# A hybrid encoder layer: the sample's first activations from a channel-major copy of the input and a tile of inverse norms, without transposes on TensorE

## Chip, cores and metric

The kernel runs on one core of one Trainium2 chip. The metric is device time in microseconds, the median of repeated executions. Engines are TensorE (PE in the profile; PEld are its weight loads), VectorE (DVE), ScalarE (ACT), GpSimd (POOL) and SyncE (SP), whose queue issues all transfers of this kernel. SBUF is the on-chip memory, PSUM the memory into which TensorE writes.

## The reference

One encoder layer is applied with the same weights to two groups: the prompt (512 tokens) and the sample (1024 tokens), each of 1024 channels in fp32. What the change touches is the first line of it, for the sample:

```python
h = rms_norm(x, g_pre_mix) * (1.0 + sc1) + sh1
u = h @ w_in
```

where `rms_norm(x, g) = x * rsqrt(mean(x*x over channels) + eps) * g`. The norm is one number per token; `g`, `sc1` and `sh1` are one number per channel. After it come five projections of `h`, a gated linear recurrence, a Fourier branch, a merge with an output projection and a residual, and then a channel sub-layer with a convolution.

## The kernel before

Products on TensorE want the contracted channels on the partitions, so `h` is held channel-major: eight tiles `h` of 128 channels x 1024 tokens for the sample. To keep fp32 accuracy each operand is split in two tiles of the type fp32r, a high part (`hh`, `ah`, and half of an `hl` weight tile) and a low part (`hl`, `al`), and each product is made of three passes: high x high, high x low, low x high (`fm_mm`, `km_mm`, `passes`). `split` (lines 105 to 112) makes the high part by a Copy on ScalarE (line 109, `act=True`) or by a cast on VectorE (line 111), and the low part by a subtract on VectorE (line 112).

The program is a list of `Step`s that `emit` (line 176) writes out in order. A step has loads, written five steps ahead of it (`LOAD_AHEAD`); a weight unit, loaded into one of three `raw` tiles and split three units ahead (`AHEAD`), into one of four `hl` tiles; the matmuls `mm`; and what follows them, `post`. `defer(fn, 1)` puts an operation to the end of the next step. The order in which each engine works is the order in which its instructions were written. A tile comes from a pool of 40 `big` buffers and is taken when one is free.

`h_steps` (line 436) makes `h` from rows of tokens in two lists of steps:

- list a, eight steps: load 128 rows (`x`), Square with a row sum on ScalarE (line 413), mean and power -0.5 on POOL (`rstd`, lines 430 and 431), and one step later the rows scaled by the inverse norm on ScalarE (`xn`, line 418).
- list b, eight steps: eight 128x128 transposes of `xn` on TensorE into PSUM (`trans`, line 204), the modulation on ScalarE (Identity with a scale and a bias per channel, line 461), the cast and the subtract on VectorE, and a store of `h` to `hrow` for the Fourier branch.

`h_steps` serves four places. The one that changes is the sample's first sub-layer. Its list a is woven into the first half of the prompt's 16 merge steps (units `w_a` and `w_b`; `weave` puts one after each), beside steps that make the gates by products on VectorE (`ada`, line 337). Its list b is woven into the prompt's eight output-projection steps (`rows_steps`, units `w_o`), one ahead of each; the texts call these R0 to R7. Ahead of each R step, three units ahead, the operands of a later one are split: activations `ah` and `al` from `mg`, and the weight tile. After R3 and after R7 four PSUM results are evicted: four Squares on ScalarE (line 1080), four products with the gate on VectorE (line 1088, `ro<-ps,gate`). Behind R7 comes the first projection of the sample, `w_xa`, 48 matmuls that walk through the eight pairs `hh`, `hl` in order; the texts call it F0. Its result goes to ScalarE at line 650.

Of the kernel before, what the change touches and what calls it, by code (L numbers as in the profile page):

```python
# [11 lines left out]
F32R = mybir.dt.float32r  # L12
AF = mybir.ActivationFunctionType
ALU = mybir.AluOpType
# [4 lines left out]
KT = D // 128  # L19
# [53 lines left out]
class Enc:  # L73
# [359 lines left out]
    def h_steps(self, sq, src, sub, box, quads=False):  # L433
        nc = self.nc
        xn = []
        box["hi"], box["lo"] = [], []
        rows = []

        def ld(t):
            def f():  # L440
                x = self.big([128, 1024], name="x")
                nc.sync.dma_start(out=x, in_=src[t * 128:(t + 1) * 128, :])
                rows.append(x)
            return f

        def norm(t):
            return lambda: xn.append(self.norm_rows(rows[t], True))

        def tr(g):
            def f():  # L450
                ps = self.ps([128, sq.nf, sq.n])
                for i in range(sq.nf):
                    k = g * sq.nf + i
                    for t in range(sq.tt):
                        self.trans(
                            ps[:, i, t * 128:(t + 1) * 128], xn[t][:, k * 128:(k + 1) * 128], self.ident)
                n = sq.n
                h = self.big([128, sq.nf, n], name="h")
                for i in range(sq.nf):
                    k = g * sq.nf + i  # L460
                    nc.scalar.activation(
                        out=h[:, i, 0:n], in_=ps[:, i, :], func=AF.Identity,
                        scale=self.gs[:, sub, sq.idx, k:k + 1], bias=self.mod[:, 3 * sub, sq.idx, k:k + 1])
                if quads:
                    blocks(h)
                    return
                hi = self.big([128, sq.nf, n], F32R, name="hh")
                lo = self.big([128, sq.nf, n], F32R, name="hl")
                self.split(hi, lo, h)
                for i in range(sq.nf):  # L470
                    box["hi"].append(hi[:, i, :])
                    box["lo"].append(lo[:, i, :])
                if sub == 0:
                    self.defer(lambda: nc.sync.dma_start(
                        out=self.hrow[sq.name][g * sq.nf:(g + 1) * sq.nf].rearrange("k p n -> p k n"), in_=h), 1)

            def blocks(h):
                for c in range(2):
                    t = self.big([128, 2, 512], F32R, name="hx")
                    self.split(t[:, 0, :], t[:, 1, :], h[:, 0, c * 512:(c + 1) * 512])  # L480
                    box.setdefault((g // 4, c), []).append(t)
            return f
        a = [Step(loads=[ld(t)], post=norm(t)) for t in range(sq.tt)]
        b = [Step(mm=tr(g)) for g in range(sq.groups)]
        return a, b


# [893 lines left out]
def weave(main, side, at, stride):  # L1381
    out = []
    side = list(side)
    for i, s in enumerate(main):
        if i >= at and (i - at) % stride == 0 and side:
            out.append(side.pop(0))
        out.append(s)
    return out + side


def place(main, side, at):
    out = []
    side = list(side)
    at = sorted(at)
    for i, s in enumerate(main):
        while at and at[0] <= i and side:
            at.pop(0)
            out.append(side.pop(0))
        out.append(s)
    return out + side  # L1400


@with_exitstack
def encoder(ctx: ExitStack, tc: tile.TileContext, a, outs):
    nc = tc.nc
    e = Enc(ctx, tc, a, outs)
    p, s = e.p, e.s
    x2 = {q.name: e.dram([q.n, D], "x2" + q.name) for q in (p, s)}
    sig = {q.name: {(w, g): e.dram([128, 1024], f"sg{q.name}{w}{g}") for w in range(2) for g in range(q.groups)}
           for q in (p, s)}  # L1410
    with tc.manual_schedule():
        e.setup()
        h1 = {"p": {}, "s": {}}
        h2 = {"p": {}, "s": {}}
        hs = {q: {} for q in "ps"}
        yb = {q: {} for q in "ps"}
        pq = {q: {} for q in "ps"}
        z = {q: {} for q in "ps"}
        mg = {q: {} for q in "ps"}
        gate = {(q, i): {} for q in "ps" for i in range(2)}  # L1420
        fo = {q: {} for q in "ps"}

        def mix(q, heads):
            at = 4
            out = heads[:at] + e.pq_steps(q, pq[q.name], heads[:at]) + heads[at:]
            out += e.ya_steps(q, h1[q.name], hs[q.name], yb[q.name])
            out += e.dft_steps(q, pq[q.name], z[q.name])
            return out

        first, heads = e.mix_heads(p, h1["p"], hs["p"], sig["p"], lead=3)  # L1430
        side = [e.cond_step()] + e.ada_steps(2) + [Step(), Step()] + e.gate_steps(p, 0, gate["p", 0])
        steps = mix(p, heads)
        ya = len(steps) - 10
        sa, sbt = e.h_steps(s, a["x_sample"], 0, h1["s"])
        steps += weave(e.merge_steps(p, yb["p"], z["p"], sig["p"], mg["p"]), sa, 1, 1)
        steps = place(steps, side, [ya - 10] + [ya - 4 + i for i in range(16)] + [ya + 13] + [ya + 22] * 9)
        steps += weave(e.rows_steps(p, a["w_o"], mg["p"], gate["p", 0], a["x_prompt"], x2["p"]), sbt, 0, 1)

        _, heads = e.mix_heads(s, h1["s"], hs["s"], sig["s"])
        steps += place(mix(s, heads), e.ada_steps(3) + e.ada_steps(4), [0, *range(8, 37), *range(36, 46)])  # L1440
        pa, pbt = e.h_steps(p, x2["p"], 1, h2["p"])
        steps += weave(e.merge_steps(s, yb["s"], z["s"], sig["s"], mg["s"]),
                       e.gate_steps(s, 0, gate["s", 0]) + pa, 8, 1)
        steps += weave(e.rows_steps(s, a["w_o"], mg["s"], gate["s", 0], a["x_sample"], x2["s"]), pbt, 4, 2)

        steps += weave(e.up_steps(p, h2["p"], fo["p"]),
                       e.ada_steps(5) + [Step()] * 2 + e.gate_steps(p, 1, gate["p", 1]), 2, 1)
        sa, sbt = e.h_steps(s, x2["s"], 1, h2["s"], quads=True)
        steps += weave(e.rows_steps(p, a["w_down"], fo["p"], gate["p", 1], x2["p"], outs[0]),
                       sa + sbt, 0, 1)  # L1450
        fs = e.dram([FT, 128, 1024], "fs")
        steps += place(e.up_quads(s, h2["s"], fs, 3), e.quad_sums(h2["s"]), [0, 1, 2, 2, 3, 3, 4, 4])
        steps += weave(e.rows_steps(s, a["w_down"], fo["s"], gate["s", 1], x2["s"], outs[1], last=True, fsrc=fs),
                       e.gate_steps(s, 1, gate["s", 1]), 4, 1)

        e.begin(steps)
        e.lead_in(p, a["x_prompt"], first, h1["p"], (2, 2, 2, 2))
        e.emit()
        e.flush()
# [31 lines left out]
def _fm(w):  # L1491
    k, m = w.shape
    return np.ascontiguousarray(w.reshape(k // 128, 128, m // 128, 128).transpose(2, 1, 0, 3)).reshape(m // 128, 128, k)
# [12 lines left out]
def layouts(i):  # L1506
    f = {k: np.asarray(v) for k, v in i.items()}
    o = {"x_prompt": f["x_prompt"][0], "x_sample": f["x_sample"][0]}
    wi = f["w_in"][0]
    o["w_xa"], o["w_ya"] = _fm(wi[:, 0:1024]), _fm(wi[:, 1024:2048])  # L1510
    o["wxbT"] = np.ascontiguousarray(wi[:, 2048:2560].T).reshape(4, 128, 1024)
# [11 lines left out]
    for g in range(GRP):  # L1523
        r = slice(63 * g, 63 * g + 63)
# [45 lines left out]
```

## Time and profile before

| | |
|---|---|
| median of 3 runs (lowest to highest) | 2103.09 us (2102.49 to 2103.74) |
| the profiled execution | 2103.23 us |
| its span, first to last instruction | 2101.1 us |
| mean granted TensorE clock | 0.997 |
| busy: PE, DVE, ACT, POOL | 2068.3, 1420.8, 944.8, 55.3 us |
| transposes of `xn` on PE in the whole kernel | 192, of which 64 belong to the place that changes |

Times in rows are in us from the start of the span. A row of a timeline has the start, the duration, engine, line, operation, output <- inputs, the tile's shape and the count of instructions merged into it; in square brackets stands the idle time of the engine just before it and what ended it. Instructions of one kind on one engine overlap a little, so the distance from start to start can be shorter than the duration.

### The profile page before, as it was taken

How to read it: one execution, taken by the hardware profiler on the slowest of the kernel's cores; microseconds unless marked ns; L12 is line 12 of the kernel's file. 1: busy time of each engine (PE TensorE's matmuls, PEld its weight loads, DVE VectorE, ACT ScalarE, POOL GpSimd, SP SyncE). 2: the span in 40 equal slices, each digit the busy share in tenths (PEclk: the TensorE clock that was granted, in tenths of full speed). 3: DMA queues.
4: the chain of work that ended last, by engine and by line, in shares of the span. 5: the costliest groups of instructions: out<-in, count | busy, mean ns of one | idle time of the engine just before them, and what ended most of it. 6: DMA issues, size and time to landing. Idle time of an engine off the chain costs nothing.

```text
span 2101.1 us, 24339 instructions
## 1 busy us (share of the span) xinstructions
PE 2068.3 (98%) x9602; PEld 1687.5 (80%) x9602; DVE 1420.8 (68%) x1798; ACT 944.8 (45%) x1213; POOL 55.3 (3%) x132
## 2 busy tenths in 40 slices
PE   7999999999999999999999999999999999999998
PEld 6777778888888888888888888888888888888887
DVE  4677888677667664656576445749687887875553
ACT  2377555355565632135333336633344444454442
POOL 0000010000000000000100001000000000000000
PEclk9999999999999999999999999999999999999999
DMA  9643475632233314343543324332122222284422
GB/s 342 206 131 130 145 259 188 236 135 96 100 105 99 112 50 145 121 146 122 217 147 116 111 96 166 100 123 88 61 76 83 83 81 81 100 313 165 143 92 109
DMA packets 91121, 284.57 MB, mean 135 GB/s; under 512 B 9056, under 2 KB 20736, under 8 KB 91008
## 3 DMA queue, kind: packets, MB, share of 16 engines
q1 hardware_dynamic: 91008, 283.03, 39.3%
q8 instruction: 75, 1.23, 0.2%
q14 instruction: 38, 0.31, 0.0%
HBM read 237.87 MB, written 45.12 MB: 135 GB/s over the span
## 4 chain that ended last, share of the span: by engine, by line
PE 87%; DVE 5%; ACT 4%; issue 2%; DMA 2%; POOL 0%; SPq 0%; DVEq 0%; POOLq 0%; ACTq 0%
PE ps L201 86%; PE ps L204 1%; DVE hl L112 1%; ACT th L684 1%; ACT th L694 1%; DVE xc L658 1%; ACT ea L692 1%; DMA hr<-hrowp 1%; ACT xn L413 0%; DVE th L715 0%; DVE th L720 0%; DVE th L718 0%; DMA x<-in_x_sample_dram 0%; DMA x<-in_x_prompt_dram 0%; ACT hl L109 0%
## 5 line engine op out<-in xcount | busy, mean ns | idle before, releaser
L201 PE MATMUL ps<-hh,hl 128*128 128x512 f32 x2144 | 632.6, 394 | 3.5 <-DVE hl L112 3.0
L201 PEld LDWEIGHTS ps<-hh,hl 128*128 128x128 f32 x2144 | 402.2, 188 | 99.5 <-DVE hl L112 4.3
L201 PE MATMUL ps<-hl,ah 128*128 128x512 f32 x1440 | 452.3, 395 | 0.0
L112 DVE TENSOR_TENSOR hl<-raw,hl 128x1024 fp32r<-128x1024 f32 (+2 forms) x240 | 286.8, 1200 | 172.3 <-ACT hl L109 170.8
L201 PE MATMUL ps<-hl,hl 128*128 128x512 f32 x1072 | 380.8, 394 | 0.0
L201 PE MATMUL ps<-hx,wq 128*128 128x512 f32 x1596 | 370.9, 394 | 0.0
L109 ACT ACTIVATE hl<-raw 128x1024 fp32r<-128x1024 f32 (+1 forms) x222 | 232.5, 1053 | 279.3 <-PE ps L201 235.2
L201 PEld LDWEIGHTS ps<-hx,wq 128*128 128x128 f32 x1596 | 299.7, 188 | 71.0 <-DVE wq L1251 0.2
L201 PEld LDWEIGHTS ps<-hl,ah 128*128 128x128 f32 x1440 | 269.0, 188 | 61.8
L201 PE MATMUL ps<-hl,al 128*128 128x512 f32 x720 | 283.9, 394 | 0.0
L201 PEld LDWEIGHTS ps<-hl,hl 128*128 128x128 f32 x1072 | 201.4, 188 | 47.6
L201 PEld LDWEIGHTS ps<-hl,al 128*128 128x128 f32 x720 | 135.2, 188 | 32.0
L1347 DVE SCALAR_TENSOR_TENSOR cf<-ps,vec,cf 128x511 f32<-128x511 f32 (+1 forms) x100 | 75.3, 808 | 83.7 <-ACT cf L1339 83.5
L201 PE MATMUL ps<-yh,hl 128*128 128x512 f32 x384 | 111.8, 394 | 0.6 <-DVE yb L991 0.3
L1250 ACT ACTIVATE wq<-wsum 128x512 fp32r<-128x512 f32 x76 | 46.1, 629 | 118.0 <-DVE wsum L1261 118.0
L1195 DVE SCALAR_TENSOR_TENSOR cf<-cq,vec,cf 128x1023 f32<-128x1023 f32 x76 | 97.1, 1277 | 0.0
L1339 ACT ACTIVATE cf<-ps,vec 128x512 f32<-128x512 f32 (+1 forms) x50 | 39.1, 827 | 105.8 <-PE ps L201 105.8
L201 PEld LDWEIGHTS ps<-yh,hl 128*128 128x128 f32 x384 | 71.5, 188 | 17.6 <-DVE yb L991 0.8
L112 DVE TENSOR_TENSOR al<-fq,ah 128x512 fp32r<-128x512 f32 x88 | 57.2, 686 | 32.3 <-PE ps L201 18.4
L201 PE MATMUL ps<-hx,hl 128*128 128x512 f32 x288 | 66.9, 394 | 0.0
L201 PE MATMUL ps<-yl,hl 128*128 128x512 f32 x192 | 65.3, 394 | 0.0
L658 DVE SCALAR_TENSOR_TENSOR xc<-ps,vec,xc 128x511 f32<-128x511 f32 (+3 forms) x48 | 46.9, 1012 | 25.7 <-ACT xc L650 25.1
(182 smaller groups left out, 2325.0 us busy)
## 6 DMA issues: line engine op xcount, KB each, us to landing
raw<-in_w_up_dram SPq DMA_DIRECT2D x88, 512.0 KB, 3.5
raw<-in_w_down_dram SPq DMA_DIRECT2D x66, 512.0 KB, 3.5
ada<-in_w_adaT_dram SPq DMA_DIRECT2D x32, 512.0 KB, 4.9
raw<-in_w_o_dram SPq DMA_DIRECT2D x24, 512.0 KB, 3.5
fs<-cf SPq DMA_DIRECT2D x22, 512.0 KB, 2.6
fq<-fs SPq DMA_DIRECT2D x22, 512.0 KB, 6.0
ada<-in_w_ada_dram SPq DMA_DIRECT2D x16, 512.0 KB, 8.5
raw<-in_w_gb_dram SPq DMA_DIRECT2D x16, 512.0 KB, 4.3
```

The costliest lines, as they stand in the source:

```text
L109: nc.scalar.activation(out=hi, in_=src, func=AF.Copy)
L112: nc.vector.tensor_tensor(out=lo, in0=src[:, 0:keep], in1=hi[:, 0:keep].bitcast(F32), op=ALU.subtract)
L201: self.nc.tensor.matmul(*args, **kw)
L204: self.nc.tensor.transpose(*args)
L658: nc.vector.scalar_tensor_tensor(out=xc[:, f, o], in0=ps[:, f, o.start + d:o.stop + d], scalar=w[:, tap:tap + 1], in1=xc[:, f, o], op0=ALU ...
L684: nc.scalar.activation(out=t[:, f, :], in_=ps[:, f, :], func=AF.Tanh, scale=0.5, bias=self.halfb[:, b:b + 1])
L692: nc.scalar.activation(out=ea[:, f, :], in_=r[:, f, :], func=AF.Exp, scale=self.nk4[:, k:k + 1], bias=self.nk4[:, k:k + 1])
L694: nc.scalar.activation(out=r[:, f, :], in_=r[:, f, :], func=AF.Tanh, scale=self.k2[:, k:k + 1], bias=self.k2[:, k:k + 1])
L1195: nc.vector.scalar_tensor_tensor(out=box[key][:, o], in0=c[:, i], scalar=self.vec[:, V_FW + 3 * m + t:V_FW + 3 * m + t + 1], in1=box[key][ ...
L1250: nc.scalar.activation(out=hi, in_=src, func=AF.Copy)
L1339: nc.scalar.activation(out=acc[:, f, :], in_=ps[:, f, :], func=AF.Identity, scale=w[:, 1:2], bias=self.vec[:, V_FB + m:V_FB + m + 1])
L1347: nc.vector.scalar_tensor_tensor(out=acc[:, f, o], in0=ps[:, f, o.start + d:o.stop + d], scalar=w[:, tap:tap + 1], in1=acc[:, f, o], op0=A ...
```

## The change

The sample's first sub-layer uses a new function, `ht_steps`, in place of `h_steps`. The host also hands over the sample transposed: `x_sampleT`, eight tiles of 128 channels x 1024 tokens.

- List a keeps load, Square (now in place) and POOL's norm. The scaling of the rows is gone. Instead the 128 norms of a tile are stored to a row in DRAM (`rrow`, elements of 4 bytes), one step later; after the last one, all 1024 norms are loaded as a tile `rb`, the same row on every partition.
- List b has no matmuls. Each of its eight steps has a load of a channel tile, five steps ahead, and as its `post`: a product with `rb` on VectorE, the modulation on ScalarE, and the split with the Copy on ScalarE (it was a cast on VectorE) and the subtract on VectorE. The store to `hrow` stays.

```diff
+        def norm(t):
+            def f():
+                ss = self.small()
+                rs[t] = self.small()
+                x = rows[t]
+                nc.scalar.activation(out=x, in_=x, func=AF.Square, accum_out=ss)
+                self.rstd(rs[t], ss)
+                self.defer(lambda: nc.sync.dma_start(out=rrow[t:t + 1, :].rearrange("o p -> p o"), in_=rs[t]), 1)
+                if t == sq.tt - 1:
+                    self.defer(back, 1)
+            return f
+
+        def back():
+            rows.clear()
+            box["r"] = self.big([128, n], name="rb")
+            nc.sync.dma_start(
+                out=box["r"], in_=rrow.rearrange("(o t) p -> o (t p)", o=1).to_broadcast([128, n]))
+
+        def ldt(k):
+            def f():
+                x = self.big([128, n], name="xt")
+                nc.sync.dma_start(out=x, in_=srcT[k])
+                cols.append(x)
+            return f
+
+        def make(k):
+            def f():
+                h = cols.pop(0)
+                nc.vector.tensor_tensor(out=h, in0=h, in1=box["r"], op=ALU.mult)
+                nc.scalar.activation(out=h, in_=h, func=AF.Identity, scale=self.gs[:, 0, sq.idx, k:k + 1],
+                                     bias=self.mod[:, 0, sq.idx, k:k + 1])
+                hi = self.big([128, n], F32R, name="hh")
+                lo = self.big([128, n], F32R, name="hl")
+                self.split(hi, lo, h, act=True)
+                box["hi"].append(hi)
+                box["lo"].append(lo)
+                self.defer(lambda: nc.sync.dma_start(out=self.hrow[sq.name][k], in_=h), 1)
...
+        a = [Step(loads=[ld(t)], post=norm(t)) for t in range(sq.tt)]
+        b = [Step(loads=[ldt(k)], post=make(k)) for k in range(KT)]
         return a, b
...
-        sa, sbt = e.h_steps(s, a["x_sample"], 0, h1["s"])
+        sa, sbt = e.ht_steps(s, a["x_sample"], a["x_sampleT"], h1["s"])
...
+    o["x_sampleT"] = np.ascontiguousarray(f["x_sample"][0].T).reshape(8, 128, 1024)
```

## Rows read from the trace of the kernel before

**Rows 1.** The page's part 1: busy time, share and instructions of the engines.

```profile
PE 2068.3 (98%) x9602; PEld 1687.5 (80%) x9602; DVE 1420.8 (68%) x1798; ACT 944.8 (45%) x1213; POOL 55.3 (3%) x132
```

**Rows 2.** Timeline of TensorE, the R steps.

```profile
335.91 1.04 PE L204 MATMUL ps<-ident,xn 128*128 128x128 f32 x8
336.70 0.71 PE L201 MATMUL ps<-hl,ah 128*128 128x512 f32 x2
...
337.48 0.62 PE L201 MATMUL ps<-hl,ah 128*128 128x512 f32 x2
...
387.45 0.62 PE L201 MATMUL ps<-hh,hl 128*128 128x512 f32 x2
```

**Rows 3.** Timeline of ScalarE: the first Square after R3, and F0's result.

```profile
360.45 0.60 ACT L1080 ACTIVATE junk<-ps 128x512 f32<-128x512 f32 x1 [2.83 <-PE ps L201]
...
398.75 1.21 ACT L650 ACTIVATE xc<-ps,vec 128x1024 f32<-128x1024 f32 x1 [8.69 <-PE ps L201]
```

**Rows 4.** Timeline of VectorE: a subtract behind ScalarE's copy, in the Fourier branch.

```profile
411.95 1.23 DVE L112 TENSOR_TENSOR el<-eo,eh 128x1024 fp32r<-128x1024 f32 x1 [1.13 <-ACT eh L109]
```

**Rows 5.** Timelines of ScalarE, VectorE, TensorE and SyncE, the merge stage.

```profile
312.53 1.15 ACT L418 ACTIVATE xn<-x,sm 128x1024 f32<-128x1024 f32 x1 [1.26 <-POOL sm L431]
...
321.65 1.06 ACT L109 ACTIVATE hl<-raw 128x1024 fp32r<-128x1024 f32 x1 [3.24 <-DMA raw<-in_w_a_dram]
322.88 1.06 ACT L109 ACTIVATE hl<-raw 128x1024 fp32r<-128x1024 f32 x1 [0.17 <-DMA raw<-in_w_a_dram]
...
314.66 1.23 DVE L112 TENSOR_TENSOR hl<-raw,hl 128x1024 fp32r<-128x1024 f32 x1 [2.85 <-ACT hl L109]
...
315.94 0.73 PE L201 MATMUL ps<-yh,hl 128*128 128x512 f32 x2 [0.29 <-DVE hl L112]
...
315.92 1.14 SPq L124 DMA_DIRECT2D raw<-in_w_a_dram  x2
```

**Rows 6.** Landing of the gate row's store (line 370), and issues by line: its broadcast load.

```profile
DMA to landing us min/median/max: 2.5/2.8/3.1
...
gate<-grow SPq DMA_DIRECT2D x4, 512.0 KB, 6.2
```

**Rows 7.** Timeline of VectorE, the R steps and after.

```profile
341.26 1.23 DVE L112 TENSOR_TENSOR al<-mg,ah 128x1024 fp32r<-128x1024 f32 x1 [1.13 <-ACT ah L109]
342.41 1.22 DVE L112 TENSOR_TENSOR hl<-raw,hl 128x1024 fp32r<-128x1024 f32 x1
343.54 0.69 DVE L111 CAST hh<-h 128x1024 fp32r<-128x1024 f32 x1
...
364.54 1.22 DVE L112 TENSOR_TENSOR al<-mg,ah 128x1024 fp32r<-128x1024 f32 x1
...
375.86 1.23 DVE L112 TENSOR_TENSOR hl<-raw,hl 128x1024 fp32r<-128x1024 f32 x1 [3.38 <-ACT hl L109]
...
422.26 3.92 DVE L658 SCALAR_TENSOR_TENSOR xc<-ps,vec,xc 128x1022 f32<-128x1022 f32 x3 [4.19 <-ACT xc L650]
```

**Rows 8.** Durations (ns) of like operations; ScalarE's timeline of two dependent ones.

```profile
L1187 ACT ACTIVATE cf<-cq,vec x38: 1227/1236/1245, 1505.0 to 1864.8; 128x1024 f32<-128x1024 f32 x38
...
L1204 DVE TENSOR_TENSOR cf<-cf,cf x19: 1214/1218/1226, 1518.1 to 1882.1; 128x1024 f32<-128x1024 f32 x19
...
727.79 1.25 ACT L694 ACTIVATE th<-th,k 128x1024 f32<-128x1024 f32 x1
729.07 1.06 ACT L696 ACTIVATE th<-th 128x1024 f32<-128x1024 f32 x1
```

**Rows 9.** Timeline of TensorE at a gap; busy, clock, DMA in 2 us slices.

```profile
289.76 0.98 PE L201 MATMUL ps<-z,hl 128*128 128x258 f32 x6 [1.86 <-DVE mg L1000]
...
290.00:292.00 2.00, 1.65 (x9) 1.18 (x9) 1.90 (x6) 2.00 (x3) 0.00 (x0) 0.79 0.83 282
292.00:294.00 2.00, 2.00 (x10) 2.00 (x11) 1.97 (x7) 0.90 (x3) 1.41 (x2) 0.50 0.93 359
294.00:296.00 2.00, 1.65 (x8) 1.08 (x8) 1.93 (x3) 1.58 (x2) 0.39 (x1) 0.86 1.01 379
```

More of the change, by code (lines that the diff above doesn't have):

```diff
@@ L484, in h_steps, with ht_steps, ld, f @@
         b = [Step(mm=tr(g)) for g in range(sq.groups)]
+        return a, b
+    def ht_steps(self, sq, src, srcT, box):
+        nc = self.nc
+        n = sq.n
+        box["hi"], box["lo"] = [], []
+        rows, cols, rs = [], [], {}
+        rrow = self.dram([sq.tt, 128], "rrow" + sq.name)
+        def ld(t):
+            def f():
+                x = self.big([128, 1024], name="x")
+                nc.sync.dma_start(out=x, in_=src[t * 128:(t + 1) * 128, :])
+                rows.append(x)
+            return f
[20 more added lines that the diff above has]
+                cols.append(x)
+            return f
+        def make(k):
+            def f():
+                h = cols.pop(0)
[8 more added lines that the diff above has]
+                self.defer(lambda: nc.sync.dma_start(out=self.hrow[sq.name][k], in_=h), 1)
+                if k == KT - 1:
+                    box.pop("r")
+            return f
+        a = [Step(loads=[ld(t)], post=norm(t)) for t in range(sq.tt)]
+        b = [Step(loads=[ldt(k)], post=make(k)) for k in range(KT)]
         return a, b
```

## The prediction, made before the change was timed

> **What bounds the kernel now.** I read the page's busy times first: TensorE is busy 98% of the span [rows 1], so what counts is its own work and its few idle gaps; what another engine does costs nothing until TensorE waits for it. Then the timelines of all engines from 280 to 430 us, the only stretch the change touches: the prompt's merge steps, the eight output-projection steps R0 to R7, and the first head step of the sample, which I call F0. In R0 to R7 TensorE shows no gap: eight times a group of eight transposes and then 24 matmuls, from 335.91 to 387.45 [rows 2]. F0 follows at 387.45, and its result is free when ScalarE starts on it, at 398.75 [rows 2, 3].
>
> The reader is to see one more thing in the timelines: VectorE and ScalarE take their instructions in the written order. VectorE's subtract at 411.95 sat idle 1.13 us for ScalarE's copy of the tile that VectorE itself had just written [rows 4]. So a tile that goes from VectorE to ScalarE and back holds up VectorE, and everything queued behind it there.
>
> **What TensorE loses.** A group of transposes takes from 335.91 to 336.70, 0.79 us, and the pair of matmuls behind it 0.71 us instead of the 0.62 of a later pair: 0.88 per group, 7.0 for the eight [rows 2]. The rest of the stretch is (51.54 - 7.04) / 8 = 5.56 us per step. Nothing replaces this work on TensorE. If all else were ready, 7.0 us would go.
>
> **The merge stage.** ScalarE drops the eight scalings of the input rows, 1.15 us each, and the wait for POOL ahead of each (1.26 in the row shown) [rows 5]. Behind that scaling stood the copy of a weight tile, and VectorE had idled 2.85 us for it. So that copy and VectorE's subtract come about 2.4 us sooner, and the 0.29 us for which TensorE waited for that subtract go [rows 5]. Some of the 2.4 is lost again: the next weight tiles come by DMA and ScalarE waits for them (3.24 and 0.17 us, at 321.65 and 322.88). On SyncE's queue there are now eight small stores of inverse norms and one broadcast load. The last store waits for POOL's last norm, the load waits for that store, and behind the load stands the second of the two w_a tiles issued at 315.92 [rows 5]. The nearest store landed in 2.5 to 3.1 us [rows 6], so this tile is issued some 1 to 3 us later than before. It is needed by TensorE only for the last merge step, so this costs at most what of the 2.4 it takes back. The broadcast itself (6.2 us by the like load of the gate [rows 6]) has some 15 us before its first use. I take VectorE to reach R3's operands, at 341.26 before [rows 7], 2.0 us earlier, at 339.3; the bounds are 3 us earlier (all gaps there close) and 2 us later (the small stores land as slowly as the gate's load).
>
> **R0 to R7: the chain.** Before, VectorE did per step: two subtracts for the weights and activations of three steps ahead, then cast and subtract of h, which ScalarE had already taken from PSUM. It ran them back to back, 1.14 apart [rows 7]. After, the same place holds: multiply (VectorE), Identity (ScalarE), Copy (ScalarE), subtract (VectorE). VectorE can't go on between multiply and subtract. Durations from rows: multiply 1.22 (the same form on two SBUF tiles), Identity with both vectors from SBUF 1.24, Copy 1.05 (1.06 at 321.65 [rows 5]), each handover 0.03; and ScalarE's second of two dependent operations begins only when the first is over (727.79 + 1.25, then 729.07) [rows 8]. Multiply to subtract is thus 1.22 + 1.24 + 1.05 + 4 x 0.03, about 3.62. With the subtract and the two subtracts of the next step, each 1.14, one step costs VectorE 7.04 us. TensorE's step is 5.56. So VectorE becomes slower than TensorE for as long as the chain lasts, and its lead of three steps pays at first.
>
> With A the start of R3's operands on VectorE: the first multiply is at A + 2.3, the fourth subtract starts at A + 27.0. Then comes the eviction after R3, whose matmuls ended long before: from ScalarE's first Square to VectorE's next free moment it took 360.45 to 364.54, 4.1 us [rows 3, 7], so A + 31.0. Two subtracts and 3.62 bring the fifth one to A + 36.9. The last three steps split one weight tile and no activations (7.04 - 1.14 = 5.9): the sixth, seventh and eighth start at A + 42.8, 48.7 and 54.6, and the last low part is ready at A + 55.8. ScalarE's Identity waits for the multiply with the next weight's Copy queued behind it; that Copy falls into VectorE's own subtract and delays nobody. SyncE's store of h waits for the Identity, and the weight loads behind it have three units' time.
>
> TensorE meanwhile would start F0 at 335.6 + 8 x 5.56 = 380.1 (R0 0.3 earlier). F0 walks the eight channel tiles in order, (398.75 - 387.45) / 8 = 1.41 us each, and would want the last tile at about 390. With A = 339.3 its high part comes at 393.9 and its low part at 395.1: TensorE waits about 3.8, then 0.8, and 0.2 for the seventh tile. This is what is late next. F0's result is then ready at 395.1 + 1.15 (four matmuls and the handover) = 396.2 instead of 398.7, so 2.5 us remain of 7.3. Operands of R4 to R7 come in time: the tightest, R7's, at A + 33.3 = 372.6 against a start near 374.5.
>
> **The clock.** A wait of that kind is not free afterwards. At 289.76 TensorE came out of 1.86 us of idling, after shorter gaps, and the granted clock was 0.79, 0.50 and 0.86 in the next three slices of 2 us: the lower level (1.2 GHz) for part of them, 0.42 + 1.0 + 0.28 = 1.7 us lost in all [rows 9]. In F0 TensorE would idle about twice as long at a stretch, so the bounds are 0 and 1.7; part of the low clock falls into the wait itself, and I take 1.2. The Trainium skill, "TensorE: Matmul & The Clock Gate", section "HAM oscillation — how this bites in real kernels", says the same against this change: a gap in TensorE's work puts it back to the lower clock and the work after it pays. By that rule the sum is -1.3; without it -2.5.
>
> **The rest.** The eviction after R7 comes behind the chain, some 8 us later than before, on both engines; two PSUM buffers are free for F0 and the step after, and VectorE idled 4.19 us ahead of 422.26 [rows 7], so I cost it at nothing; if that cover failed, up to 1 us. The transposed copy of the input is 4 MB of loads on a queue whose transfers are not the limit here, in buffers that the scaled rows used to hold: nothing.
>
> **The sum.** -7.0 (transposes) - 0.3 (merge gap) + 4.8 (F0's waits; 0.2 + 3.8 + 0.8) + 1.2 (clock) = -1.3 us. Against the profiled execution's 2103.23 (span 2101.1 and 2.1 around it), which is 0.1 above the median of 2103.09: 2102.0.
>
> **Rivals.** (1) *The chain stays hidden.* Then 7.3 us go: 2095.9. It needs the last low part some 5 us earlier than I have it, at 390. For it: TensorE never waited for VectorE in this stretch before, and VectorE had gaps of about 3 us per step in R5 to R7 (3.38 at 375.86) [rows 7]. Against it: those gaps close only if VectorE may run ahead, and here it stands and waits for ScalarE in each step. Halfway results (the hand-overs shorter by 0.3 a step, VectorE a us further ahead) end near 2099.
>
> (2) *SyncE and the clock make it slower.* One mechanism: the queue stands at the broadcast load until the 4-byte stores have landed; the w_a tile behind it is late, ScalarE stands at its copy, and VectorE reaches R3's operands later than before. Every us of A goes into F0's end one for one, and the clock loss is full at 1.7. With A = 343.3 F0's result comes at 400.3, 1.6 later than before, and with 1.7 on top the time is 2106.5. It decides from A = 340.1 on with the full clock loss. For it: ScalarE already waited 0.17 us for that very tile [rows 5]. Against it: the small store of the gate rows landed in 3.1 us at most [rows 6], and ScalarE gains 2.4 us before.
>
> (3) *The clock doesn't fall*, with the chain as I have it: 2103.2 - 2.5 = 2100.7.
>
> **How the numbers follow.** Forecast with A between 338.3 and 341.3 and a clock loss of 0 to 1.7 (rival 3 is its lower part): own range 2099.5 to 2105, chance 0.6. Rival 1 with its halfway results 0.2, rival 2 0.2. The range for eight times in ten reaches half way into rival 1 and to rival 2's point: 2097 to 2106.5. About 0.2%, 4.2 us, is what a measurement of this kernel can tell from no change. Faster by more than that, under 2098.9: most of rival 1 and a sliver of the forecast, 0.22. Slower by more, over 2107.3: the half of rival 2 beyond its point, and little of the forecast, 0.12. Within: 0.66.
>
> **What would show it.** No transposes from 335 to 390, and R steps of 5.56 us. On VectorE, an idle of about 2.4 us ahead of each subtract of h, released by ScalarE's Copy, and a step of 7 us. On TensorE, a wait of 3 to 4 us inside F0 for the copy of the eighth tile, then 0.8 for its subtract, and granted clock at half after it. Wrong would be: no wait in F0 (rival 1), R4 or R7 waiting for operands, or R3's operands on VectorE later than 341.3 (rival 2).

## The result, and the profile after

| | before | after |
|---|---|---|
| median of 4 runs each (lowest to highest) | 2103.16 us (2102.49 to 2103.74) | 2126.92 us (2126.31 to 2130.32) |
| ratio, 95% interval | | 1.0115, 1.0103 to 1.0127 |
| span of the profiled execution | 2101.1 us | 2124.2 us |

The changed kernel is slower by 23.8 us. The forecast of 2102.0 is wrong, and the range, which ended at 2106.5, does not hold the time.

The page's head and its chain of waits (the work that ended last, followed back) show that TensorE still bounds the kernel: it is busy for 2075.6 us, 7 more than before [rows 1], although it has 64 transposes less to do. The low clock described below lengthens its matmuls: a pair takes 1.22 us at 417.41 and 0.62 at 401.68.

```profile
PE 2075.6 (98%) x9538; PEld 1687.8 (79%) x9538; DVE 1424.7 (67%) x1798; ACT 945.0 (44%) x1213; POOL 54.1 (3%) x132
...
PE 83%; DVE 6%; ACT 4%; DMA 3%; issue 3%; SPq 0%; POOL 0%; DVEq 0%; POOLq 0%; ACTq 0%
```

**Where the time went.** TensorE's timeline of the changed kernel, from the merge stage to the first head step F0 (columns as in the rows of before):

```profile
323.05 0.50 PE L201 MATMUL ps<-yh,hl 128*128 128x512 f32 x1 [2.13 <-ACT hl L109]
...
341.28 0.80 PE L201 MATMUL ps<-yh,hl 128*128 128x512 f32 x1 [6.89 <-ACT hl L109]
...
355.21 0.62 PE L201 MATMUL ps<-hl,ah 128*128 128x512 f32 x2
...
396.21 0.50 PE L201 MATMUL ps<-hl,ah 128*128 128x512 f32 x1 [1.20 <-DVE hl L112]
...
401.68 0.62 PE L201 MATMUL ps<-hh,hl 128*128 128x512 f32 x2
...
411.52 0.73 PE L201 MATMUL ps<-hh,hl 128*128 128x512 f32 x2 [1.31 <-ACT hh L109]
...
417.41 1.22 PE L201 MATMUL ps<-hh,hl 128*128 128x512 f32 x2 [3.12 <-ACT hh L109]
```

R0 starts at 355.21; before it was 335.91 [rows 2]. The lead-in up to the merge stage is 0.8 shorter in this execution, so the merge stage alone costs 20.1 us. From R0 to ScalarE's start on F0's result (420.94 below, 398.75 before [rows 3]) it is 65.73 us instead of 62.84, so 2.9 more. The span is longer by 23.1; the last 0.9 comes behind F0's result, where the clock is still low (0.50 from 420 to 422).

TensorE's waits in the merge stage (the view of waits, 285.5 to 355.3; us in total, times, longest):

```profile
PE ps L201 <- ACT hl L109: 9.0, 2, 6.9
PE ps L201 <- DVE hl L111: 2.5, 3, 1.7
PE ps L201 <- DVE mg L1059: 1.8, 1, 1.8
PE ps L201 <- DVE hl L112: 1.5, 5, 0.5
PE ps L201 <- DVE yb L1050: 0.6, 2, 0.3
```

They sum to 15.4 us, against 3.7 before in the same stretch, so 11.7 of the 20.1 are waits. Most of the rest is the clock, which is low after the longer ones. The stage in stretches of 5 us (start:end, length, busy us of PE, PEld, DVE, ACT and POOL, granted clock, DMA share, GB/s); the first row is the kernel before, the others are the changed kernel:

```profile
290.00:295.00 5.00, 4.39 (x20) 3.47 (x19) 4.84 (x13) 3.48 (x6) 1.79 (x2) 0.66 0.91 339
...
290.00:295.00 5.00, 4.25 (x17) 3.41 (x18) 4.83 (x11) 2.24 (x4) 0.74 (x2) 0.66 1.13 75
...
310.00:315.00 5.00, 4.66 (x16) 3.40 (x17) 3.33 (x6) 1.99 (x3) 0.74 (x2) 0.61 0.89 100
315.00:320.00 5.00, 5.00 (x17) 3.98 (x16) 0.92 (x1) 0.00 (x0) 0.00 (x0) 0.71 0.97 105
...
325.00:330.00 5.00, 5.00 (x17) 3.94 (x16) 4.73 (x9) 1.06 (x3) 1.05 (x2) 0.69 1.69 335
...
335.00:340.00 5.00, 0.00 (x0) 0.00 (x0) 0.00 (x0) 0.00 (x0) 0.00 (x0) 0.84 0.18 64
340.00:345.00 5.00, 3.68 (x8) 2.48 (x9) 3.58 (x3) 1.06 (x1) 0.00 (x0) 0.50 0.61 95
```

Before, only 290 to 295 was below full clock here, at 0.66, as it is now. The new low stretches lose (0.39 + 0.29 + 0.31) x 5, and from 341.28 to 345 half of 3.7: about 7 us. With the waits that makes some 18.5 of the 20.1. The last two columns show the transfers: from 290 to 295 the DMA engines are no less busy than before (1.13 against 0.91) and move 75 GB/s instead of 339.

ScalarE's waits name who is late: the scaling of the input rows is gone, but the loads beside the stores come late. From ScalarE's timeline:

```profile
320.91 1.06 ACT L507 ACTIVATE x<-x 128x1024 f32<-128x1024 f32 x1 [8.63 <-DMA x<-in_x_sample_dram]
...
340.17 1.06 ACT L109 ACTIVATE hl<-raw 128x1024 fp32r<-128x1024 f32 x1 [14.11 <-DMA raw<-in_w_a_dram]
...
420.94 1.20 ACT L709 ACTIVATE xc<-ps,vec 128x1024 f32<-128x1024 f32 x1
```

The loads themselves (view of DMA issues; KB each, median us from issue to landing, that is to the arrival of the last byte; `sg` are the merge's gate tiles), and the stores of norms (line 509):

```profile
x<-in_x_sample_dram SPq DMA_DIRECT2D x8, 512.0 KB, 9.1
sg<-sgp SPq DMA_DIRECT2D x8, 512.0 KB, 11.5
...
DMA to landing us min/median/max: 8.2/11.2/15.4
```

The same loads of `x` and `sg` took 5.0 and 5.6 before. On SyncE's queue the last store goes out at 326.83 and the broadcast load at 340.98; the queue stands between them (view of waits, SyncE):

```profile
SPq L517 <- DMA rrows<-sm: 13.8, 1, 13.8
...
324.68 0.41 SPq L124 DMA_DIRECT2D raw<-in_w_a_dram  x1
```

This looks like rival 2's picture, but the second row speaks against it: the next `w_a` load after it goes out only at 341.39, so the tile that ScalarE copies at 340.17 went out at 324.68, ahead of the stand, and was some 15 us under way. The experiments ask whether that 13.8 us stand is the price, or the stores themselves.

### The profile page after: what moved, and what is told of

Same layout as the page of the kernel before. It is cut to its first block, busy times and chain, and to the rows that moved or that the text cites. A ratio compares the mean times of both kernels' runs of the same rounds, so it can differ in the third digit from the quotient of the medians.

```text
span 2124.2 us, 24237 instructions
## 1 busy us (share of the span) xinstructions
PE 2075.6 (98%) x9538; PEld 1687.8 (79%) x9538; DVE 1424.7 (67%) x1798; ACT 945.0 (44%) x1213; POOL 54.1 (3%) x132
## 4 chain that ended last, share of the span: by engine, by line
PE 83%; DVE 6%; ACT 4%; DMA 3%; issue 3%; SPq 0%; POOL 0%; DVEq 0%; POOLq 0%; ACTq 0%
PE ps L201 83%; DVE hl L112 2%; DMA x<-in_x_sample_dram 1%; PE ps L204 1%; DMA rrows<-sm 1%; ACT th L753 1%; ACT th L743 1%; ACT ea L751 1%; DMA hr<-hrowp 1%; DVE th L774 0%; DVE th L779 0%; DVE th L777 0%; ACT xt L531 0%; DVE al L112 0%; DVE xt L530 0%
## 5 line engine op out<-in xcount | busy, mean ns | idle before, releaser
L201 PE MATMUL ps<-yh,hl 128*128 128x512 f32 x384 | 116.8, 408 | 10.5 <-ACT hl L109 9.0
L201 PEld LDWEIGHTS ps<-yh,hl 128*128 128x128 f32 x384 | 73.9, 195 | 30.9 <-ACT hl L109 10.1
L201 PEld LDWEIGHTS ps<-hx,hl 128*128 128x128 f32 x288 | 54.1, 188 | 12.7
```

The costliest lines, as they stand in the source:

```text
L201: self.nc.tensor.matmul(*args, **kw)
```

## The experiments

The theory: the eight stores of 4-byte elements are slow and slow all transfers beside them; without them the time comes near the forecast. Rival a: the price is SyncE's stand at the broadcast load. Rival b: the chain between VectorE and ScalarE is longer than predicted and pushes TensorE.

**e1, no stores.** The changed kernel without the stores of norms; the tile `rb` is loaded from a row of the input `c`, so the norms are left out of the result.

```diff
-self.defer(lambda: nc.sync.dma_start(out=rrow[t:t + 1, :].rearrange("o p -> p o"), in_=rs[t]), 1)
-    out=box["r"], in_=rrow.rearrange("(o t) p -> o (t p)", o=1).to_broadcast([128, n]))
+    out=box["r"], in_=self.a["c"][0:1, :].to_broadcast([128, n]))
```

> The changed kernel (2126.9) without the eight stores of inverse norms; the broadcast tile is loaded from an input row of the same size instead (the norms are left out of the sample's first activations). Theory S: the eight 4-byte-element stores cost the merge stage its 20 us, by standing in the transfers' way and by making SyncE's queue wait for their landing; R0 starts near 335.5 again instead of 355.2, VectorE's start on R3's operands comes near 340, F0 still waits 4 to 6 us and the clock falls after it: 2102 to 2106. Rival L: the extra 4.5 MB of loads (transposed input and broadcast tile) fill the transfers; then little changes, over 2115. Rival C: VectorE's chain costs most of it; then over 2115 too, with R0 early and F0 late.

Measured: 2102.56 us, against 2103.6 of the kernel before on the same chip, ratio 0.9995 (0.9985 to 1.0005); `x` lands in 5.0 us and `sg` in 5.9. All of the loss is gone. TensorE, VectorE and ScalarE of e1:

```profile
335.34 0.62 PE L201 MATMUL ps<-hl,ah 128*128 128x512 f32 x2
...
380.05 0.62 PE L201 MATMUL ps<-hh,hl 128*128 128x512 f32 x2
...
339.15 1.23 DVE L112 TENSOR_TENSOR al<-mg,ah 128x1024 fp32r<-128x1024 f32 x1 [1.13 <-ACT ah L109]
...
393.68 1.23 DVE L112 TENSOR_TENSOR hl<-xt,hh 128x1024 fp32r<-128x1024 f32 x1 [2.40 <-ACT hh L109]
393.70 1.22 PE L201 MATMUL ps<-hh,hl 128*128 128x512 f32 x2 [3.44 <-ACT hh L109]
...
397.23 1.20 ACT L707 ACTIVATE xc<-ps,vec 128x1024 f32<-128x1024 f32 x1
```

A, the start of R3's operands on VectorE, is 339.15 (forecast 339.3); the eighth subtract starts at 393.68 (393.9); F0's wait for the eighth tile is 3.44 (3.8; the expectation had said 4 to 6 for F0's waits). The chain is as forecast, and rival b falls.

**e2, a broadcast load that waits for no store.** The second edit of e1 alone: the stores stay, the broadcast load reads `c` and waits for none of them, so the norms are left out here too.

> The changed kernel with its eight stores, but the broadcast tile is loaded from an input row, so that SyncE never waits for the stores to land (the norms are left out of the sample's first activations). If the price is SyncE's 13.8 us wait at the broadcast load: the wait of 6.9 us on TensorE at 341 goes, with its low clock, 2108 to 2115. If the price is what the stores do to the transfers of others (the w_a tile issued before the wait took 15.4 us to land): 2119 to 2127.

Measured: 2127.59, ratio 1.0112 (1.0097 to 1.0127), so as slow as the changed kernel. The stores land in 10.1 to 16.6 us, `x` in 10.3 and `sg` in 11.9, and TensorE waits even longer for the weight tile:

```profile
346.09 0.80 PE L201 MATMUL ps<-yh,hl 128*128 128x512 f32 x1 [9.46 <-ACT hl L109]
```

Rival a falls: without SyncE's stand at the broadcast load the kernel is no faster. e2 does not take away every wait for a store: the view of waits puts 4.7 us of SyncE ahead of a load of `xt` down to one.

**e3, the kernel before with the stores added.** They are read by nobody.

```diff
+self.defer(lambda: nc.sync.dma_start(out=rrow[t:t + 1, :].rearrange("o p -> p o"), in_=rs), 1)
```

> The kernel before with the eight stores added in the same places, read by nobody; nothing is left out. If the stores by themselves slow the other transfers: 2110 to 2122, with gaps on TensorE between 295 and 345 behind weight tiles that land late. If they cost only through the wait for them: 2103 to 2104.

Measured: 2128.32, ratio 1.0118 (1.0103 to 1.0133). These 4 KB of stores alone cost the kernel before 24.7 us, more than the 2110 to 2122 that the expectation had for this case. Its DMA issues, and one stretch of its stage:

```profile
rrows<-sm SPq DMA_DIRECT2D x8, 0.5 KB, 13.1
x<-in_x_sample_dram SPq DMA_DIRECT2D x8, 512.0 KB, 10.7
...
290.00:295.00 5.00, 4.69 (x19) 3.92 (x19) 4.83 (x11) 3.48 (x6) 1.80 (x2) 0.50 1.16 72
```

**e4, the subtract of h two steps later,** to break the chain in the changed kernel.

```diff
-self.split(hi, lo, h, act=True)
+nc.scalar.activation(out=hi, in_=h, func=AF.Copy)
+self.defer(lambda: nc.vector.tensor_tensor(out=lo, in0=h, in1=hi.bitcast(F32), op=ALU.subtract), 2)
```

> The changed kernel with the subtract of each h tile written two steps later, behind the next tile's multiply, so that VectorE doesn't stand between multiply and subtract; stores as in the changed kernel. Chain theory: VectorE's step falls from 7.04 to about 4.6 us, F0's waits (5.0) and the low clock after them (414 to 423, some 4.6 lost) go: 2117 to 2119, R0 still at 355. Rival: VectorE is late only because the merge stage is late, and F0 waits as before: 2125 to 2127.

Measured: 2135.68, ratio 1.0153 (1.0138 to 1.0169): a miss, 17 us above the expected range and 8.8 slower than the changed kernel. Of these 8.8, 3.4 arise ahead of the edited steps, as R0 starts at 358.58 and not at 355.21. From R0 to ScalarE's start on F0's result it takes 70.68 us against 65.73, so the new order itself costs 5. The loop between the engines only moved. Two steps of ScalarE and VectorE, and F0's last wait:

```profile
369.77 1.25 ACT L531 ACTIVATE xt<-xt,mod,gs 128x1024 f32<-128x1024 f32 x1 [2.61 <-DVE xt L530]
...
376.62 1.25 ACT L531 ACTIVATE xt<-xt,mod,gs 128x1024 f32<-128x1024 f32 x1 [2.62 <-DVE xt L530]
379.94 1.22 DVE L112 TENSOR_TENSOR al<-mg,ah 128x1024 fp32r<-128x1024 f32 x1 [2.22 <-ACT ah L109]
...
427.14 1.22 PE L201 MATMUL ps<-hl,hl 128*128 128x512 f32 x2 [5.86 <-DVE hl L536]
```

ScalarE's Identity waits 2.6 for the multiply; the multiply stands behind VectorE's split of the next operands; that split waits 2.2 for ScalarE's Copy of those operands, which stands behind Identity and Copy of this tile. The step is 376.62 - 369.77 = 6.85, hardly less than 7.04, and each low part comes later than in the changed kernel, where no subtract was put off.

**What makes the stores dear: f1 to f4 and h1.** f1 to f4 add stores to the kernel before as e3 does; h1 is e2, norms left out as there, with the pieces apart. Of each edit the place and source of the store are shown; a piece is what one partition writes:

```diff
 f1: 128 pieces of 512 bytes, eight times
+out=rrow[t], in_=rows[t][:, 0:128]
 f2, h1: 128 pieces of 4 bytes, 512 bytes apart in DRAM (rrow is [8, 128, 128])
+out=rrow[t][:, 0:1], in_=rs
 f4: the same, 64 bytes apart (rrow is [8, 128, 16])
+out=rrow[t][:, 0:1], in_=rs
 f3: one store of all eight norms per partition, 128 pieces of 32 bytes
+out=rrow, in_=box["rs"]
```

> The kernel before with eight added stores, each of 128 pieces of 512 bytes (a slice of the input rows) to separate places, in the places where e3 had eight stores of 128 pieces of 4 bytes; nothing is left out. e3 took 2128.3 against 2103.6. If the number of pieces makes the price: 2120 or more. If their size does: 2103 to 2106, landing in 2 to 4 us.

> The kernel before with the eight stores of 128 pieces of 4 bytes, each piece 512 bytes away from the next one in DRAM instead of beside it; nothing is left out. If pieces of 4 bytes are slow wherever they go: 2120 to 2130, as e3. If the price is that neighbours go to one place of DRAM at the same time: 2103 to 2108.

> The kernel before with one added store of all norms, 128 pieces of 32 bytes (eight norms of a partition), after the last norm; nothing is left out. By an eighth of e3's price (24.7 us): 2104 to 2107. If pieces of 32 bytes are cheap as such: 2103 to 2104; if one store alone already holds up the transfers for its landing of 8 to 15 us: 2108 to 2115.

> The kernel before with the eight stores of 128 pieces of 4 bytes, each piece 64 bytes from the next (512 bytes apart cost nothing: 2104.0; side by side they cost 24.7 us: 2128.3); nothing is left out. If pieces get in each other's way only within a few tens of bytes: 2103 to 2105. If within a few hundred: between 2106 and 2125.

> e2 (2127.6: the changed kernel with its eight stores, the broadcast tile loaded from an input row, so the norms are left out) with each stored piece of 4 bytes 512 bytes from the next. If the closeness of the pieces is the whole of the extra cost in the changed kernel too: as e1, 2101 to 2105. If something else of the stores costs there (SyncE waiting for POOL ahead of each): over 2108.

| stores | median, us | ratio, 95% interval | median landing of a store, us |
|---|---|---|---|
| e3: 8 x 128 x 4 bytes, side by side | 2128.32 | 1.0118 (1.0103 to 1.0133) | 13.1 |
| f4: the same, 64 bytes apart | 2104.38 | 1.0005 (0.9996 to 1.0014) | 5.3 |
| f2: the same, 512 bytes apart | 2104.0 | 1.0002 (0.9993 to 1.0012) | 4.7 |
| f1: 8 x 128 x 512 bytes | 2104.62 | 1.0003 (0.9994 to 1.0013) | 5.6 |
| f3: 1 x 128 x 32 bytes | 2103.28 | 1.0000 (0.9991 to 1.0009) | 4.1 |
| e2: the changed kernel, side by side, unread | 2127.59 | 1.0112 (1.0097 to 1.0127) | 13.0 |
| h1: the same, 512 bytes apart | 2103.8 | 1.0002 (0.9993 to 1.0011) | 4.6 |

f2, f4 and h1 fall in the ranges expected if neighbouring pieces are the price, f1 and f3 in those for cheap pieces of 512 and 32 bytes; only f1's stores landed later than expected, in 5.6 us and not in 2 to 4. The count of pieces, their 4 bytes and the count of stores are the same in e3, f2 and f4, and so are the place in the program and the packets that the page counts on the queue (92160). What differs is the distance at which the pieces lie in DRAM, and with it 24 us. DMA issues of f2 and the same stretch as in e3:

```profile
rrows<-sm SPq DMA_DIRECT2D x8, 0.5 KB, 4.7
x<-in_x_sample_dram SPq DMA_DIRECT2D x8, 512.0 KB, 4.6
...
290.00:295.00 5.00, 4.20 (x19) 3.30 (x19) 4.84 (x11) 3.49 (x6) 1.79 (x2) 0.70 0.90 320
```

In this stretch the DMA engines move 320 GB/s where they moved 72. f3 says nothing of 32-byte pieces in number, since it has one store and not eight. The distance between 4 and 64 bytes at which it begins was not tried. With the distance grows the stretch of DRAM that a store covers (512 bytes, 8 KB, 64 KB), and the runs don't tell the two apart. Why the chip does it stays open.

The Trainium skill, "DMA: Bandwidth & Descriptors", section "Why small descriptors are slow (HBM only)", puts the price of small transfers on two fixed costs, one per packet and one of descriptor metadata per DMA operation. By these alone e3, f2 and f4, with pieces equal in number and size, would take the same time; they differ by 24 us, so what e3 pays on top is not what that section describes.

**g1, g3 and g4: the change with other ways for the norms and another order.** g1 turns the norms into rows by one 128x8 transpose on TensorE, six steps after the last norm, and stores eight rows of 512 bytes; the broadcast load stays.

```diff
+ps = self.ps([8, 128])
+self.trans(ps, rs["all"], self.ident)
+nc.scalar.activation(out=sb, in_=ps, func=AF.Copy)
+nc.sync.dma_start(out=rrow, in_=sb)
```

> The changed kernel with the norms turned to a row by one 128x8 transpose on TensorE, copied by ScalarE, and stored as eight pieces of 512 bytes, then loaded as the broadcast tile; nothing is left out. Theory (small pieces made the price, the rest of my sum holds): as e1 (2102.6), 2100 to 2105, with F0 waiting 4 to 6 us behind the chain. Rival: the wait for the norms, now on TensorE and SyncE late in the merge stage, costs as much: over 2108.

g3 is g1 with the multiply one tile ahead and the subtract one tile behind (`mult` is VectorE's product with `rb`, `sub` the subtract; the last tile's `sub` is not put off):

```diff
+if k == 0:
+    mult(0)
+if k < KT - 1:
+    mult(k + 1)
 ... (Identity and Copy of tile k on ScalarE)
+self.defer(sub, 2)
```

> g1 (2103.8: norms as a row by one transpose, eight pieces of 512 bytes) with VectorE's multiply written one tile ahead and its subtract one tile behind, so that neither engine stands for the other inside a tile; nothing is left out. Chain theory: VectorE's step falls from 7.04 to about 4.6 us, under TensorE's 5.56; F0's wait and the low clock after it go: 2096 to 2099. Rival (the order doesn't matter, ScalarE's queue is the limit, as e4 with only the subtract moved seemed to say): 2102 to 2105.

g4 has g3's order, and no DRAM in it: POOL scales the identity by each column of norms, and eight matmuls with ones put the rows on all partitions.

```diff
+nc.gpsimd.tensor_scalar(out=box["d"][:, t, :], in0=self.ident, scalar1=rs[t], scalar2=None, op0=ALU.mult)
+self.mmul(ps[:, t // 4, t % 4 * 128:t % 4 * 128 + 128], lhsT=self.ones, rhs=d[:, t, :], start=True, stop=True)
```

> As g3, but the tile of norms is made on chip: POOL scales the identity by each column of norms, TensorE multiplies a tile of ones with it (eight matmuls of 128 columns in fp32), ScalarE copies the result from PSUM; no store and no load for the norms; nothing is left out. Chain theory: 2096 to 2100; the eight fp32 matmuls cost TensorE up to 2 us more than g3's one transpose, against SyncE's wait for the row, which it drops.

Measured: g1 2103.82, ratio 0.9999 (0.9989 to 1.0008), with 3.4 us of wait in F0; g3 2097.78, 0.9975 (0.9965 to 0.9985); g4 2097.4, 0.9974 (0.9964 to 0.9983). g3 and g4 are faster than both kernels, by 0.25% of the kernel before. g1's wait in F0 (view of waits), then g3's VectorE, a stretch of its R steps, and ScalarE's start on F0's result:

```profile
PE ps L201 <- ACT hh L109: 3.4, 1, 3.4
...
347.20 1.22 DVE L538 TENSOR_TENSOR xt<-xt,rb 128x1024 f32<-128x1024 f32 x1
348.33 1.22 DVE L554 TENSOR_TENSOR hl<-xt,hh 128x1024 fp32r<-128x1024 f32 x1
...
351.74 1.22 DVE L538 TENSOR_TENSOR xt<-xt,rb 128x1024 f32<-128x1024 f32 x1
...
336.00:388.00 52.00, 52.00 (x226) 42.05 (x225) 43.92 (x43) 36.82 (x46) 7.39 (x12) 1.00 0.89 317
...
390.21 1.21 ACT L731 ACTIVATE xc<-ps,vec 128x1024 f32<-128x1024 f32 x1 [8.74 <-PE ps L201]
```

The multiply of one tile and the subtract of another stand back to back, the step is 4.54 us and so shorter than TensorE's 5.56, TensorE does not wait in F0, and its clock stays full. g1 and g3 have the same stores and the same load of `rb`; between them lie 5 to 6 us (by the ratios, and by the medians), which is what the chain in its written order takes from the change. From R0 to ScalarE's start on F0's result the traces have 61.88 us in g1 and 55.99 in g3.

## Why the prediction was wrong

**The step that failed is the landing of the small stores,** in the part on the merge stage: it took them by the nearest store, 2.5 to 3.1 us, and saw their only price in the weight tile behind the broadcast load. That nearest store, of line 370, writes 16 rows of 512 bytes; the new ones write 128 pieces of 4 bytes side by side, and by f1 and f2 it is neither 512-byte pieces nor lone 4-byte pieces that cost. They took 8.2 to 15.4 us to land, at the median four times as much, and the price was not in the queue's stand: e2, without it, is as slow. While they are under way the loads of `x` and `sg` take about twice as long. Rival 2 had the right sign and the right suspect, with the wrong mechanism and hence the wrong size: it set A = 343.3 by the queue's stand alone, where 362.85 was measured. The bound on A (2 us later) let the stores land as slowly as the gate's load; no bound allowed a small store to slow other transfers. The term for the merge stage was thus forecast at -0.3 and measured at +20.1. (In e1, without the stores, the stage takes 49.76 us from the wait at 285.58 to R0, against 49.59 from the same wait before, so the -0.3 can't be seen there either. And 2103.23 - 1.3 is 2101.9, where the forecast says 2102.0; that has no weight.)

**The transposes** (-7.0): right. In e1 the eight R steps take 44.7 us (335.34 to 380.05), forecast 8 x 5.56 = 44.5.

**The chain** (step of 7.04, 2.4 us of idle ahead of each subtract): right. The changed kernel itself, VectorE:

```profile
362.85 1.22 DVE L112 TENSOR_TENSOR al<-mg,ah 128x1024 fp32r<-128x1024 f32 x1 [1.13 <-ACT ah L109]
...
368.76 1.23 DVE L112 TENSOR_TENSOR hl<-xt,hh 128x1024 fp32r<-128x1024 f32 x1 [2.40 <-ACT hh L109]
...
375.80 1.23 DVE L112 TENSOR_TENSOR hl<-xt,hh 128x1024 fp32r<-128x1024 f32 x1 [2.40 <-ACT hh L109]
...
417.39 1.23 DVE L112 TENSOR_TENSOR hl<-xt,hh 128x1024 fp32r<-128x1024 f32 x1 [2.39 <-ACT hh L109]
```

375.80 - 368.76 = 7.04, and A + 54.6 gives 417.45 for the eighth subtract.

**F0's waits** (0.2 + 3.8 + 0.8): in e1 the wait for the eighth tile is 3.44 and the one for its low part is gone: with the clock at half the two matmuls ahead of it take 1.22 us (at 393.70), as long as the subtract beside them. In the changed kernel R7 waits 1.20 besides, which the prediction named as a sign of error: VectorE reaches R3's operands 7.64 us after R0's start (362.85 - 355.21) instead of 3.81 in e1, so 3.8 us of its lead were lost in the merge stage. By as much R0 to F0's result is longer than in e1 (65.73 against 61.89).

**The clock** (+1.2, bounds 0 to 1.7): too small. e1 from 392 to 400, in stretches of 2 us as above:

```profile
392.00:394.00 2.00, 0.30 (x1) 0.30 (x2) 0.32 (x1) 1.97 (x3) 0.00 (x0) 0.63 0.89 344
394.00:396.00 2.00, 1.96 (x5) 1.05 (x5) 1.93 (x3) 1.91 (x7) 1.08 (x3) 0.50 0.33 135
...
398.00:400.00 2.00, 2.00 (x7) 1.53 (x7) 2.00 (x4) 1.38 (x2) 2.00 (x2) 0.66 0.06 11
```

396 to 398 is at 0.50 too. That is (0.37 + 0.50 + 0.50 + 0.34) x 2 = 3.4 us below full clock, of which the first 0.7 falls mostly into the wait. So about 2.7 stand against the 1.2, and the missing wait for the low part, 0.8, pays back some of it. With no stores the whole comes out at -1.0 (2102.56 against 2103.6), forecast -1.3. The interval of that ratio reaches from -3.2 to +1.1 us, so it can't confirm the sum to a microsecond, and that a clock taken too cheap and a wait taken too dear partly cancel is luck.

**Rivals 1 and 3**: both fall, as TensorE waits in F0 and its clock falls. Most of the 7.3 us that rival 1 gave are there, though: g3 and g4, where the chain is hidden, reach 2097.8 and 2097.4, some 6 us below the kernel before; rival 1's price was 2095.9.

## What to carry to other kernels

A small store is not priced by its own landing alone: ask what else is on the DMA engines at that time, and lay 4-byte pieces out apart in DRAM (64 bytes were enough here; a load that reads such pieces back was not run) or turn them into rows on the chip first. Where a tile goes from VectorE to ScalarE and back, write the first operation one tile ahead and the last one tile behind; to move only one of them can make it worse (e4). And a resource that the trace of before doesn't show, here stores of 4-byte pieces, deserves a range as wide as everything it could slow.

## What was not expected of the hardware

Eight stores of 512 bytes each, in pieces of 4 bytes side by side in DRAM, hold the transfers to 72 GB/s at a DMA share of 1.16 (290 to 295 in e3), where the same pieces 512 bytes apart leave them at 320 GB/s at 0.90 (f2). They cost 24.7 us, and those 64 bytes apart 0.9, an amount whose interval includes zero.

TensorE lost about twice as much to the low clock around the 3.44 us wait in e1 (3.4 us, some 0.7 of it inside the wait) as behind the 1.86 us gap that the forecast went by (1.7 us [rows 9]).
